# Output projection with stationary weights for 800 of its 1056 tokens

## The chip, the cores and the metric

The kernel runs on one core of a Trainium2 chip. The metric is the device time of one execution in microseconds (us); the less the better. TensorE (PE) does the matrix products, VectorE (DVE) and ScalarE (ACT) work on vectors, GpSimd (POOL) does a few element-wise operations and issues transfers, SyncE (SP) only issues transfers. PE reads a stationary operand, loaded ahead (PEld), and a moving one that streams past it, and writes to a PSUM bank of 128 partitions of 512 fp32.

## What is computed

One layer of a hybrid decoder trunk: 1024 prompt tokens and 8 x 4 = 32 sample tokens, 1056 in all, model width 1024. The end of the reference is what matters here:

```
pa = (oa * silu(ga)) @ w_proj_a      # likewise pb, pc
m = sigmoid(ma) * pa + sigmoid(mb) * pb + sigmoid(mc) * pc
hp = x + m @ w_out                   # the output projection, 1024 x 1024
y = hp * rsqrt(mean(hp * hp, axis=-1) + 1e-6) * final_norm_w
```

All is fp32. The kernel gets there with matmuls of a faster type: a matrix is split into a high part (rounded) and a low part (the rest), and a product is the sum of three: high by high, low by high, high by low.

## The kernel before

The kernel has 34 blocks of an input projection with attention and pooling beside them, then eight blocks j of 128 model columns for gates, branch products and merge, then the output projection. What runs is in the order in which it is written: each engine has its own row of instructions and follows it strictly.

In block j, gates come from `proj_chunk` (L307) in the three token pieces of `CH`, 0 to 383, 384 to 767 and 768 to 1055 (0, 384 and 768 in what follows), ACT making each a tanh (L1216, `mth`). `branch` (L1207) multiplies the branch values into a bank "s" or "t", by turns; there are two banks of each, three of "pj" and one of "o", and a bank comes free when its last reader is through. `merge_add` reads that bank on DVE (L1222), and POOL adds the outcome to the sum `m` (L1224). The last block is j = 7, its last branch br = 2: its three merges complete `m` for the eighth 128 columns.

`out_load` fetches one of the eight pieces k of the weights (`wo_raw`, 128 x 1024), `out_split` makes its high half on ACT (L1236) and its low half on DVE (L1237). Pieces 5, 6 and 7 are split after the last block. `m_split` (L1242) does the same for the tokens of `m`: copy on ACT (L1246, `mh`), difference on DVE (L1247, `ml`).

The output projection goes over nine token tiles, eight of 128 and one with the 32 sample tokens. The tokens are stationary, the weights stream by in 512 columns: 8 pieces k x 3 products x 2 halves are 48 matmuls for a tile (`out_mm`, L1342), into a bank "pj" and a bank "s". The last tile takes its columns as 512, 256 and 256, one after the other. Then DVE adds the residual (`out_part`, L1347), ACT squares with a running sum along the row (L1348), POOL makes the power of -1/2 of the mean (L1374), DVE scales by that and by the norm's weights (L1381), and SP stores.

Of the kernel before, what the change touches and what calls it, by code (L numbers as in the profile page):

```python
# [96 lines left out]
def build(tc, x_p, x_s, w_in, w_pr, w_out, nw, fnw, sink, sinkrow, w_pool, pscale, st_a, st_b1, st_b2, st_b3, st_c,  # L97
          kt_a, kt_b1, kt_b2, kt_b3, ct, c_bias, c_sb, c_pw,
          y_p, y_s, a_p, a_s, b1_p, b1_s, b2_p, b2_s, b3_p, b3_s, cp_o, cs_o):
# [1150 lines left out]
    for j in range(8):  # L1250
# [69 lines left out]
    m_split(1, range(8))  # L1320
    parts = ((mh, 0), (ml, 0), (mh, 1))
    for ti, i in enumerate(tiles):
        rows = 128 if i < 8 else NS
# [21 lines left out]
        def out_part(n, c0, cn):  # L1345
            cs = slice(c0, c0 + cn)
            dve.tensor_tensor(out=xr[:rows, cs], in0=xr[:rows, cs], in1=banks[c0][:rows, :cn], op=ALU.add)  # L1347
            act.activation(out=sq[:rows, cs], in_=xr[:rows, cs], func=AF.Square, accum_out=ss[:rows, n:n + 1])  # L1348

        dst = y_p[t0:t0 + 128, :] if i < 8 else y_s  # L1350
        if last:
            for n, (c0, cn) in enumerate(((0, 512), (512, 256), (768, 256))):
                for k in range(8):
                    for si in range(3):
                        out_mm(k, si, c0, cn)
                out_part(n, c0, cn)
                if n == 0:
                    pool.tensor_tensor(out=xr[:rows, 0:512], in0=xr[:rows, 0:512], in1=fw[:rows, 0:512], op=ALU.mult)
# [112 lines left out]
```

## Time and profile before

| | |
|---|---|
| median of 3 runs | 1087.18 us (1085.97 to 1088.93) |
| the profiled execution's own time | 1084.24 us |
| its span in the profile | 1082.5 us |
| mean granted clock of PE | 0.99 |
| busy: PE, DVE, ACT, POOL | 1045.4, 435.5, 343.9, 195.8 us |
| last gate on ACT starts | 969.37 us |
| output projection on PE | 971.98 to 1072.35 us |
| last store issued by SP | 1075.36 us |

All positions are microseconds from the start of the span. A clock of 1.00 is the upper of PE's two levels, 2.4 GHz, 0.50 the lower, 1.2 GHz. Busy shares are averages over the whole run; what a step is worth has to be read from its own stretch. On PE a matmul's own duration overlaps with that of its neighbours, so the distance from start to start is what it takes of the row.

### The profile page before, as it was taken

What the parts mean: (1) busy time and instruction counts of PE and PEld (TensorE: products, weight loads), DVE (VectorE), ACT (ScalarE), POOL (GpSimd) and SP (SyncE); (2) the same over time, 40 slices, a digit from 0 to 9 for tenths busy, and PEclk for the clock granted to TensorE, in tenths of its full rate; (3) what the DMA queues carried; (4) which work ended last, traced back from release to release, by engine and by line L of the source; (5) the groups of instructions that cost most, each with busy time, mean ns of one, the idle gap of its engine ahead of it and who ended that gap; (6) DMA issues with size and microseconds to landing.
All of it is one profiled execution on the core that took longest, in us unless ns stands there. A gap on an engine that the chain in (4) does not pass through costs nothing.

```text
span 1082.5 us, 18049 instructions
## 1 busy us (share of the span) xinstructions
PE 1045.4 (97%) x7421; PEld 994.4 (92%) x7421; DVE 435.5 (40%) x960; ACT 343.9 (32%) x888; POOL 195.8 (18%) x303
## 2 busy tenths in 40 slices
PE   7999999999999999979999899999999999999996
PEld 7998999999999999968979899999999999998884
DVE  5656654544435343474224641222122221346331
ACT  5456543544535244222211311111112121243221
POOL 5400030211303030300003460311113021111011
PEclk8999999999999999999999999999999999999998
DMA  7241133425254453527568853454143240332221
GB/s 258 79 161 59 60 126 115 149 71 184 70 176 131 124 179 113 160 80 260 194 235 208 256 167 117 164 167 136 60 135 131 83 159 33 92 116 89 100 83 58
DMA packets 54574, 144.42 MB, mean 133 GB/s; under 512 B 13030, under 2 KB 29732, under 8 KB 53156
## 3 DMA queue, kind: packets, MB, share of 16 engines
q1 hardware_dynamic: 41980, 65.28, 19.5%
q0 software_dynamic: 2816, 44.87, 12.2%
q10 hardware_dynamic: 9696, 33.12, 9.9%
q8 instruction: 58, 0.95, 0.4%
q14 instruction: 24, 0.20, 0.1%
HBM read 127.65 MB, written 60.55 MB: 174 GB/s over the span
## 4 chain that ended last, share of the span: by engine, by line
PE 83%; DMA 7%; DVE 5%; ACT 2%; POOL 1%; SPq 1%; issue 1%; POOLq 0%; ACTq 0%; DVEq 0%
PE ps_pj L307 53%; PE ps_pj L1342 5%; PE ps_s L1342 4%; PE ps_s L1207 4%; PE ps_t L1207 4%; PE ps_s L505 3%; PE ps_o L547 3%; PE ps_t L525 2%; DMA w_in<-w_scr 2%; POOL o_in L1134 1%; DMA w_raw<-in_w_in 1%; DMA w_in<-rz_scr 1%; DMA kv<-in_kt_b 1%; PE ps_o L860 1%; DMA o_in<-o_scr 1%
## 5 line engine op out<-in xcount | busy, mean ns | idle before, releaser
L307 PE MATMUL ps_pj<-xh,w_hi 128*128 128x384 f32 (+2 forms) x1408 | 461.7, 335 | 6.4 <-ACT xh L295 3.0
L307 PE MATMUL ps_pj<-xh,w_lo 128*128 128x384 f32 (+2 forms) x1408 | 443.9, 322 | 5.2 <-DVE w_lo L150 5.1
L307 PE MATMUL ps_pj<-xl,w_hi 128*128 128x384 f32 (+2 forms) x1408 | 444.4, 322 | 0.0
L307 PEld LDWEIGHTS ps_pj<-xh,w_hi 128*128 128x128 f32 x1408 | 263.2, 190 | 16.1 <-issue 6.3
L307 PEld LDWEIGHTS ps_pj<-xh,w_lo 128*128 128x128 f32 x1408 | 261.6, 188 | 6.4 <-DVE w_lo L150 6.0
L307 PEld LDWEIGHTS ps_pj<-xl,w_hi 128*128 128x128 f32 x1408 | 262.7, 189 | 0.7 <-issue 0.3
L150 DVE TENSOR_TENSOR w_lo<-w_raw,w_hi 128x1024 fp32r<-128x1024 f32 x55 | 67.3, 1224 | 204.6 <-ACT w_hi L149 197.0
L1216 ACT ACTIVATE mth<-ps_pj 128x384 f32<-128x384 f32 (+1 forms) x72 | 33.4, 464 | 257.3 <-PE ps_pj L307 250.3
L1224 POOL TENSOR_TENSOR m<-m,mth 128x384 f32<-128x384 f32 (+1 forms) x48 | 47.8, 1012 | 275.4 <-DVE mth L1222 274.9
L397 POOL TENSOR_SCALAR k<-k 64x384 fp32r<-64x384 f32 (+1 forms) x44 | 20.1, 458 | 298.4 <-ACT k L393 298.1
L512 ACT ACTIVATE e<-e,nm_b 128x256 f32<-128x256 f32 (+1 forms) x96 | 44.2, 461 | 62.9 <-DVE nm_b L509 62.6
L149 ACT ACTIVATE w_hi<-w_raw 128x1024 fp32r<-128x1024 f32 x57 | 60.1, 1054 | 1.0 <-DMA w_raw<-in_w_in 1.0
L357 DVE SCALAR_TENSOR_TENSOR q<-ps_pj,q 64x384 fp32r<-64x384 f32 (+1 forms) x60 | 30.7, 512 | 60.2 <-ACT q L356 60.1
L505 PE MATMUL ps_s<-k,q 128*128 128x256 f32 x320 | 51.6, 285 | 0.9 <-DVE nm_a L509 0.9
L505 PEld LDWEIGHTS ps_s<-k,q 128*128 128x128 f32 x320 | 45.9, 188 | 1.3 <-issue 1.2
L525 PE MATMUL ps_t<-ident,e 128*128 128x128 f32 x276 | 42.9, 273 | 1.8 <-ACT pt L530 1.1
L1134 POOL TENSOR_TENSOR o_in<-o_in,w_in 128x1024 f32<-128x1024 f32 x10 | 27.9, 2795 | 86.8 <-DMA o_in<-o_scr 62.8
L356 ACT ACTIVATE q<-ps_pj 64x384 fp32r<-64x384 f32 (+1 forms) x60 | 26.8, 447 | 50.4 <-PE ps_pj L307 29.3
L182 POOL DMA_DIRECT2D out_b_s<-in_st_b x84 | 42.2, 507 | 0.0
L512 ACT ACTIVATE e<-e,nm_a 128x256 f32<-128x256 f32 (+1 forms) x64 | 31.1, 487 | 27.9 <-DVE nm_a L509 27.9
L509 DVE CUSTOM_DVE_ANT_0 e<-ps_s,bias 128x256 f32<-128x256 f32 (+1 forms) x96 | 31.9, 371 | 14.9 <-PE ps_s L505 14.2
L525 PEld LDWEIGHTS ps_t<-ident,e 128*128 128x128 f32 x276 | 33.8, 140 | 4.3 <-ACT pt L530 1.9
(240 smaller groups left out, 1323.4 us busy)
## 6 DMA issues: line engine op xcount, KB each, us to landing
out_b_s<-in_st_b POOLq DMA_DIRECT2D x64, 511.0 KB, 6.8
w_raw<-in_w_in ACTq DMA_DIRECT2D x55, 512.0 KB
kv<-in_kt_b SPq DMA_DIRECT2D x16, 512.0 KB
kv<-in_st_b SPq DMA_DIRECT2D x16, 512.0 KB
out_b_s<-in_st_b POOLq DMA_DIRECT2D x16, 508.0 KB, 5.2
o_scr<-os SPq DMA_DIRECT2D x20, 256.0 KB
o_in<-o_scr SPq DMA_DIRECT2D x10, 512.0 KB
x_nat<-in_x_p SPq DMA_DIRECT2D x8, 512.0 KB
```

What stands on the lines that cost most here:

```text
L149: act.activation(out=hi, in_=raw, func=AF.Copy)
L150: eng.tensor_tensor(out=lo, in0=raw, in1=hi.bitcast(F32), op=ALU.subtract)
L182: pool.dma_start(out=dst, in_=src)
L307: pe.matmul(ps[:, :cn], lhsT=parts[p][0][:, k, :], rhs=parts[p][1][:, k, c0:c0 + cn], start=(step == 0), stop=(step == 23))
L505: pe.matmul(ps[:, 256 * hd:256 * hd + 256], lhsT=q, rhs=rhs, start=(i == 0), stop=(i == 1))
L512: act.activation(out=e[:, hd, :nk], in_=e[:, hd, :nk], func=AF.Exp, scale=-1.0, bias=nm, accum_out=z)
L525: pe.transpose(tp[:, o:o + 128], e[:, hd, 128 * k:128 * k + 128], ident)
L1134: pool.tensor_tensor(out=t[:, :L], in0=t[:, :L], in1=w[:, :L], op=ALU.mult)
L1207: pe.matmul(pp[:, :cn], lhsT=a[:, k, :], rhs=b[k][:, c0:c0 + cn], start=(step == 0), stop=(step == last))
L1216: act.activation(out=th[:, :cn], in_=ps[:, :cn], func=AF.Tanh, scale=0.5)
L1224: pool.tensor_tensor(out=dst, in0=dst, in1=th[:, :cn], op=ALU.add)
L1342: pe.matmul(banks[c0][:rows, :cn], lhsT=a[:, k, t0:t0 + rows], rhs=wo[k][b][:, c0:c0 + cn], start=(k == 0 and si == 0), stop=(k == 7 and s ...
```

## The change

Tokens are now in four pieces `OC`: c = 0 is tokens 768 to 1055 (288 columns, the 32 sample tokens among them), c = 1 is tokens 0 to 511, and two pieces of 128 make up the last 256.

For c = 0 and 1 the weights are stationary and the tokens stream by: for an output block o of 128 model columns, 24 matmuls (L1392) of 288 or 512 columns fill one bank. Groups of c = 0 are o = (0, 1) in the two banks "s", (2, 3, 4) in the three "pj", then 5, 6 and 7 alone in "pj"; c = 1 takes one o at a time. The result stands transposed, model columns on partitions. So the residual `x_t` comes in transposed (`x_res`), the outcome leaves as `y_t` and the host turns it back (`hand_back`). The norm is a sum over partitions: ACT squares, POOL adds the eight o up (`acc`, L1349), PE multiplies by a column of ones (L1357), DVE makes the mean, POOL the power (L1362), PE spreads it over the partitions through the identity (L1368, `spread`), ACT copies it out, DVE scales (`out_store`, L1377). The last 256 tokens go as two token tiles (L1430) like those before; the last of them, now with 128 rows and not 32, has columns 512, 256 and 256.

The low and high halves of weights 5, 6 and 7 are made earlier, in block 7, in other buffers. The last three merges go in reversed order, 768 first. The tokens' split goes by pieces of `OC`, and its first seven parts stand ahead of those merges.

```diff
+        hi = p1.tile([128, 1024], F32R, tag=t1_, name=f"wo_hi{k}", **({"bufs": 2} if p1 is wr else {}))
+        lo = p2.tile([128, 1024], F32R, tag=t2_, name=f"wo_lo{k}", **({"bufs": 2} if p2 is wr else {}))
...
+    OC = ((768, 288), (0, 512), (512, 128), (640, 128))
+
+    def m_split(c, ks):
+        s = slice(OC[c][0], OC[c][0] + OC[c][1])
         for k in ks:
             act.activation(out=mx[0][:, k, s], in_=m_t[k][:, s], func=AF.Copy)
             dve.tensor_tensor(out=mx[1][:, k, s], in0=m_t[k][:, s], in1=mx[0][:, k, s].bitcast(F32), op=ALU.subtract)
...
                 r[7] = out_load(7, wr, "whi", bufs=2)
+                out_split(5, r[5], wr, "wlo", wr, "raw")
...
+                if j == 7 and br == 2 and ci == 1:
+                    out_split(7, r[7], gh, "h3", gl, "l3")
...
                 mx[:] = [mh, ml]
+                out_split(6, r[6], wr, "wlo", wr, "whi")
+                m_split(0, range(7))
...
-            for (c0, cn), th in zip(CH, ths):
+            pieces = list(zip(CH, ths))
+            for (c0, cn), th in pieces[::-1] if j == 7 and br == 2 else pieces:
                 merge_add(j, bi, c0, cn, th, branch(n0 + 1, c0, cn, br))
-                if j == 7 and br == 2 and c0 == 0:
-                    m_split(0, range(8))
+                if j == 7 and br == 2 and c0 == 768:
+                    m_split(0, [7])
...
-    out_split(5, r[5], gc1, "c0", gc2, "d0")
-    out_split(6, r[6], gc1, "c1", gc2, "d1")
-    out_split(7, r[7], gh, "h3", gl, "l3")
...
+    fw = const.tile([128, 8], F32, name="fw")
+    sp.dma_start(out=fw, in_=fnw_t)
...
+    res, acc, rs_t = {}, {}, {}
+
+    def x_res(c, places):
+        c0, cn = OC[c]
+        o = sum(1 for k in res if k[0] == c)
+        for pl, tag, n in places:
+            t = pl.tile([128, n, cn], F32, tag=tag, name="x_res", **({"bufs": 2} if pl is wr else {}))
+            sp.dma_start(out=t, in_=x_t[o:o + n, :, 288 * c:288 * c + cn].rearrange("o p t -> p o t"))
+            for i in range(n):
+                res[c, o] = t[:, i, :], t, o - i, i == n - 1
+                o += 1
+
+    def out_add(c, o, ps):
+        c0, cn = OC[c]
+        x = res[c, o][0]
+        dve.tensor_tensor(out=x, in0=x, in1=ps[:, :cn], op=ALU.add)
+        if o == 0:
+            acc[c] = const.tile([128, 512], F32, tag="reuse", name="acc")
+            act.activation(out=acc[c][:, :cn], in_=x, func=AF.Square)
+        else:
+            q = sq2[:, o % 2, :cn]
+            act.activation(out=q, in_=x, func=AF.Square)
+            pool.tensor_tensor(out=acc[c][:, :cn], in0=acc[c][:, :cn], in1=q, op=ALU.add)
+
+    def out_norm(c):
+        c0, cn = OC[c]
+        n = -(-cn // 128)
+        ps = bank("o")
+        for i in range(n):
+            m = min(128, cn - 128 * i)
+            pe.matmul(ps[:m, i:i + 1], lhsT=acc[c][:, 128 * i:128 * i + m], rhs=ones, start=True, stop=True)
+        st = const.tile([128, 8], F32, tag="fst", name="fst", bufs=2)
+        pool.memset(st[:, 0:n], 1.0)
+        for r_, i0, i1 in ((128, 0, n),) if cn % 128 == 0 else ((128, 0, n - 1), (NS, n - 1, n)):
+            dve.tensor_scalar(out=st[:r_, i0:i1], in0=ps[:r_, i0:i1], scalar1=1.0 / D, scalar2=EPS, op0=ALU.mult, op1=ALU.add)
+        pool.tensor_tensor(out=st[:, 4:4 + n], in0=st[:, 0:n], in1=mhalf.to_broadcast([128, n]), op=ALU.pow)
+
+        def spread():
+            rp = bank("t")
+            for i in range(n):
+                m = min(128, cn - 128 * i)
+                pe.matmul(rp[:, 128 * i:128 * i + m], lhsT=st[:m, 4 + i:5 + i].to_broadcast([m, 128]), rhs=ident[:m, :m], start=True, stop=True)
+            rs_t[c] = rs2[:, c % 2, :cn]
+            act.activation(out=rs_t[c], in_=rp[:, :cn], func=AF.Copy)
+
+        return spread
...
+    def out_store(c, o):
+        c0, cn = OC[c]
+        x, t, o0, full = res[c, o]
+        dve.scalar_tensor_tensor(out=x, in0=x, scalar=fw[:, o:o + 1], in1=rs_t[c], op0=ALU.mult, op1=ALU.mult)
+        if full:
+            sp.dma_start(out=y_t[o0:o + 1, :, 288 * c:288 * c + cn].rearrange("o p t -> p o t"), in_=t)
+
+    x_res(0, [(gc1, "c0", 3), (gc1, "c1", 3), (gc2, "d0", 2)])
+    x_res(1, [(gc2, "d1", 2)])
+    spread = None
+    for c in range(2):
+        c0, cn = OC[c]
+        groups = [(0, 1), (2, 3, 4), (5,), (6,), (7,)] if c == 0 else [(o,) for o in range(8)]
+        for gi, group in enumerate(groups):
+            ps = {o: bank("s" if len(group) == 2 else "pj") for o in group}
+            for k in range(8):
+                for si, (a, b) in enumerate(parts):
+                    for o in group:
+                        pe.matmul(ps[o][:, :cn], lhsT=wo[k][b][:, 128 * o:128 * o + 128], rhs=a[:, k, c0:c0 + cn],
+                                  start=(k == 0 and si == 0), stop=(k == 7 and si == 2))
+            if c == 0 and gi < 4:
+                m_split(1, range(2 * gi, 2 * gi + 2))
+            if c == 1 and gi in (5, 6):
+                m_split(gi - 3, range(8))
+            for o in group:
+                out_add(c, o, ps[o])
+            if c == 0 and gi == 1:
+                x_res(1, [(wr, "raw", 2)])
+            if c == 1 and gi == 0:
+                spread = out_norm(0)
+                x_res(1, [(wr, "whi", 2)])
+            if c == 1 and gi == 1:
+                spread()
+            if c == 1 and 1 <= gi <= 4:
+                out_store(0, 2 * gi - 2)
+                out_store(0, 2 * gi - 1)
...
+    for i in range(2):
+        xr.append(slot_tile(i, "x_tok"))
+        sp.dma_start(out=xr[i][:, :D], in_=x_p[512 + 128 * i:640 + 128 * i, :])
+    for i in range(2):
+        t0 = 512 + 128 * i
+        last = i == 1
...
+        cols = ((0, 512), (512, 256), (768, 256)) if last else ((0, 512), (512, 512))
+        banks = [bank("pj"), bank("s"), bank("pj")][:len(cols)]
...
+        def tok_mm(n, k, si):
+            a, b = parts[si]
+            c0, cn = cols[n]
+            pe.matmul(banks[n][:, :cn], lhsT=a[:, k, t0:t0 + 128], rhs=wo[k][b][:, c0:c0 + cn],
+                      start=(k == 0 and si == 0), stop=(k == 7 and si == 2))
...
-        banks = {0: bank("pj"), 512: bank("s")}
-        if last:
-            banks[768] = bank("t")
...
-        def out_mm(k, si, c0, cn):
-            a, b = parts[si]
-            pe.matmul(banks[c0][:rows, :cn], lhsT=a[:, k, t0:t0 + rows], rhs=wo[k][b][:, c0:c0 + cn],
-                      start=(k == 0 and si == 0), stop=(k == 7 and si == 2))
...
+                    for n in range(2):
+                        tok_mm(n, k, si)
+            spread = out_norm(1)
+            for n in range(2):
+                tok_part(n)
...
+        if not last:
+            spread()
+            for o in range(8):
+                out_store(1, o)
...
+def hand_back(res):
+    y = np.asarray(res["y_t"]).reshape(D, 800).T
+    y_p = np.concatenate([y[288:], np.asarray(res["y_p"]), y[:256]]).reshape(1, L, D)
+    return (y_p, y[256:288].reshape(8, 4, D)) + tuple(res[name].reshape(full) for name, _, full in _OUTS[2:])
```

On DVE, at the end of block 7, the row of the kernel before has a merge, the splits of 128 columns, then the other two merges and a weight split:

```order
L1237 TENSOR_TENSOR wo_lo4_9297<-wo_raw_9231,wo_hi4_9296 128x1024
L1222 SCALAR_TENSOR_TENSOR mth01_6458<-mth01_6458,ps_s_9384 128x384
L1247 TENSOR_TENSOR ml_9383<-m_0_6221,mh_9382 128x128
...
L1247 TENSOR_TENSOR ml_9383<-m_7_9028,mh_9382 128x128
L1222 SCALAR_TENSOR_TENSOR mth01_6458<-mth01_6458,ps_t_9409 128x384
L1222 SCALAR_TENSOR_TENSOR mth2_6459<-mth2_6459,ps_s_9418 128x288
L1237 TENSOR_TENSOR wo_lo5_9428<-wo_raw_9259,wo_hi5_9427 128x1024
```

In the changed kernel the same place on DVE reads (`m_0` to `m_7` are the eight blocks of `m`):

```order
L1237 TENSOR_TENSOR wo_lo7_9361<-wo_raw_9302,wo_hi7_9360 128x1024
L1237 TENSOR_TENSOR wo_lo6_9393<-wo_raw_9300,wo_hi6_9392 128x1024
L1248 TENSOR_TENSOR ml_9391<-m_0_6221,mh_9390 128x288
...
L1248 TENSOR_TENSOR ml_9391<-m_6_8669,mh_9390 128x288
L1222 SCALAR_TENSOR_TENSOR mth2_6459<-mth2_6459,ps_s_9410 128x288
L1248 TENSOR_TENSOR ml_9391<-m_7_9028,mh_9390 128x288
L1222 SCALAR_TENSOR_TENSOR mth01_6458<-mth01_6458,ps_t_9421 128x384
L1222 SCALAR_TENSOR_TENSOR mth01_6458<-mth01_6458,ps_s_9430 128x384
```

The low half of weight 6 and seven splits now stand ahead of all three merges, and the merges of pieces 384 and 0 behind the eighth split.

On PE, from the last branch products into the output projection, the kernel before has:

```order
L1207 MATMUL ps_s_9418<-ghi7_5563,p_hi_9029 128x288
L1207 MATMUL ps_s_9418<-glo7_5564,p_hi_9029 128x288
L1207 MATMUL ps_s_9418<-ghi7_5563,p_lo_9030 128x288
L1342 MATMUL ps_pj_9461<-wo_hi0_9195,mh_9382 128x512
L1342 MATMUL ps_s_9462<-wo_hi0_9195,mh_9382 128x512
```

And the changed kernel, in the same place:

```order
L1207 MATMUL ps_s_9430<-ghi6_5435,p_hi_9029 128x384
L1207 MATMUL ps_s_9430<-glo6_5436,p_hi_9029 128x384
L1207 MATMUL ps_s_9430<-ghi6_5435,p_lo_9030 128x384
L1207 MATMUL ps_s_9430<-ghi7_5563,p_hi_9029 128x384
L1207 MATMUL ps_s_9430<-glo7_5564,p_hi_9029 128x384
L1207 MATMUL ps_s_9430<-ghi7_5563,p_lo_9030 128x384
L1392 MATMUL ps_s_9453<-mh_9390,wo_hi0_9195 128x288
L1392 MATMUL ps_s_9454<-mh_9390,wo_hi0_9195 128x288
```

The first matmuls of the output projection went to one bank "pj" and one "s"; they now go to the two banks "s", which hold the branch products `ps_s_9410` and `ps_s_9430` that DVE's first and last merge read.

On PE, between the last two token tiles, the changed kernel has (before, a tile's last matmul is followed by the next tile's first):

```order
L1430 MATMUL ps_s_9989<-wo_lo7_9361,mh_9390 128x512
L1357 MATMUL ps_o_10039<-ones_9441,acc_9721 128x1 x4
L1368 MATMUL ps_t_10059<-ident_71,fst_10044 128x128 x4
L1430 MATMUL ps_pj_10079<-wo_hi0_9195,mh_9390 128x512
L1430 MATMUL ps_pj_10079<-wo_hi0_9195,ml_9391 128x512
```

The sums of squares of c = 1 and the spreading of its norm came in there, four small products each.

## Rows read from the trace of the kernel before

**Rows 1.** Page, part 2: PE's busy tenths in 40 equal slices.

```profile
PE   7999999999999999979999899999999999999996
```

**Rows 2.** Stretch 1000 to 1020: us, busy (count) by engine, clock, DMA share, GB/s.

```profile
core 0: us, PE busy (x) PEld busy (x) DVE busy (x) ACT busy (x) POOL busy (x), PEclk, DMA share, GB/s
1000.00:1020.00 20.00, 20.00 (x88) 16.18 (x87) 6.20 (x18) 5.55 (x23) 1.86 (x6) 1.00 0.30 95
```

**Rows 3.** Timeline of PE: start, us, line, out<-in, count [idle before <-releaser].

```profile
965.92 0.29 PE L307 MATMUL ps_pj<-xh,w_hi 128*128 128x288 f32 x1
...
969.11 0.34 PE L1207 MATMUL ps_s<-ghi,p_hi 128*128 128x384 f32 x1
...
971.98 0.39 PE L1342 MATMUL ps_pj<-wo_hi,mh 128*128 128x512 f32 x1
...
1061.19 0.39 PE L1342 MATMUL ps_pj<-wo_hi,mh 128*32 128x512 f32 x1
...
1066.73 0.28 PE L1342 MATMUL ps_s<-wo_hi,mh 128*32 128x256 f32 x1
...
1072.23 0.28 PE L1342 MATMUL ps_t<-wo_lo,mh 128*32 128x256 f32 x1
```

**Rows 4.** Timeline of ACT from the weights' splits to the last gate.

```profile
952.03 1.05 ACT L1236 ACTIVATE wo_hi<-wo_raw 128x1024 fp32r<-128x1024 f32 x1
...
966.18 0.49 ACT L1216 ACTIVATE mth<-ps_pj 128x384 f32<-128x384 f32 x1 [3.72 <-PE ps_pj L307]
...
969.37 0.41 ACT L1216 ACTIVATE mth<-ps_pj 128x288 f32<-128x288 f32 x1 [2.70 <-PE ps_pj L307]
969.67 1.50 ACT L1246 ACTIVATE mh<-m 128x128 fp32r<-128x128 f32 x7
```

**Rows 5.** Timeline of DVE: weight split, merges, token splits, and the last scalings.

```profile
953.12 1.22 DVE L1237 TENSOR_TENSOR wo_lo<-wo_raw,wo_hi 128x1024 fp32r<-128x1024 f32 x1 [2.99 <-ACT wo_hi L1236]
...
970.43 0.56 DVE L1222 SCALAR_TENSOR_TENSOR mth<-mth,ps_s 128x384 f32<-128x384 f32 x1 [7.91 <-ACT mh L1246]
...
973.81 0.44 DVE L1222 SCALAR_TENSOR_TENSOR mth<-mth,ps_s 128x288 f32<-128x288 f32 x1
...
978.93 3.31 DVE L1247 TENSOR_TENSOR ml<-m,mh 128x128 fp32r<-128x128 f32 x16
...
1064.55 1.41 DVE L1381 SCALAR_TENSOR_TENSOR sq_o<-x_res,fss,fw 128x512 f32<-128x512 f32 x2 [2.12 <-POOL fss L1374]
```

**Rows 6.** Timeline of POOL: the first of the last merges' additions, and one power.

```profile
971.13 1.13 POOL L1224 TENSOR_TENSOR m<-m,mth 128x384 f32<-128x384 f32 x1 [10.84 <-DVE mth L1222]
...
1030.51 0.55 POOL L1374 TENSOR_TENSOR fss<-fss,mhalf 128x1 f32<-128x1 f32 x1
```

**Rows 7.** Groups by shape, POOL, 880 to 1083: count | busy us, mean ns | idle before.

```profile
L1224 POOL TENSOR_TENSOR m<-m,mth 128x288 f32<-128x288 f32 x5 | 6.0, 1200 | 0.0
```

**Rows 8.** Timeline of PE, two matmuls after an idle time of over 2 us.

```profile
611.18 0.69 PE L307 MATMUL ps_pj<-xh,w_lo 128*128 128x384 f32 x1 [2.12 <-DVE w_lo L150]
...
632.68 0.44 PE L307 MATMUL ps_pj<-xh,w_lo 128*128 128x384 f32 x1 [2.29 <-DVE w_lo L150]
```

**Rows 9.** Stretches of 1 us from 611: us, PE busy, clock, DMA share, GB/s.

```profile
611.00:612.00 1.00, 0.82 (x3) 0.59 0.82 229
...
614.00:615.00 1.00, 1.00 (x6) 0.71 0.86 147
```

**Rows 10.** Timeline of PE and its loads: small loads of transposes, a plain fp32 product.

```profile
300.74 0.53 PEld L525 LDWEIGHTS ps_t<-ident,e 128*128 128x128 f32 x4
...
484.27 0.36 PEld L943 LDWEIGHTS ps_t<-diff,wpl 128*128 128x128 f32 x2
...
484.44 0.65 PE L943 MATMUL ps_t<-diff,wpl 128*128 128x288 f32 x2
```

**Rows 11.** Stretches of 0.5 us: us, PE busy, clock, DMA share, GB/s.

```profile
965.00:965.50 0.50, 0.50 (x5) 1.00 0.41 164
...
1067.00:1067.50 0.50, 0.50 (x7) 1.00 1.01 385
...
1076.50:1077.00 0.50, 0.00 (x0) 0.50 0.67 148
```

More of the change, by code (lines that the diff above doesn't have):

```diff
@@ L1240, in build @@
     mx = []
-    def m_split(i, ks):
-        rows = 128 if i < 8 else NS
-        s = slice(128 * i, 128 * i + rows)
+    OC = ((768, 288), (0, 512), (512, 128), (640, 128))
+    def m_split(c, ks):
+        s = slice(OC[c][0], OC[c][0] + OC[c][1])
         for k in ks:
@@ new lines, in build @@
+    fw = const.tile([128, 8], F32, name="fw")
+    sp.dma_start(out=fw, in_=fnw_t)
+    ones = const.tile([128, 1], F32, name="ones")
+    pool.memset(ones, 1.0)
+    sq2 = mp.tile([128, 2, 512], F32, tag="phi", name="sq_o")
+    rs2 = mp.tile([128, 2, 512], F32, tag="plo", name="rs_o")
+    parts = ((mh, 0), (ml, 0), (mh, 1))
+    res, acc, rs_t = {}, {}, {}
[8 more added lines that the diff above has]
+                o += 1
@@ new lines, in out_store @@
+    def out_store(c, o):
[33 more added lines that the diff above has]
+                out_store(0, 2 * gi - 1)
+            if c == 1 and gi == 2:
+                x_res(1, [(gc1, "c0", 2)])
@@ new lines, in build, with tok_part @@
+    fwb = slot_tile(4, "fw_b")
+    sp.dma_start(out=fwb[:, :D], in_=bass.AP(tensor=fnw.tensor, offset=fnw.offset, ap=[[0, 128], [1, 1024]]))
+    xr = []
+    for i in range(2):
[4 more added lines that the diff above has]
+        last = i == 1
+        x = xr[i]
+        sq = slot_tile(2 + i, "sq_tok")
+        ss = const.tile([128, 6], F32, tag="fss", name="fss", bufs=2)
+        cols = ((0, 512), (512, 256), (768, 256)) if last else ((0, 512), (512, 512))
[5 more added lines that the diff above has]
+                      start=(k == 0 and si == 0), stop=(k == 7 and si == 2))
+        def tok_part(n):
+            c0, cn = cols[n]
+            cs = slice(c0, c0 + cn)
+            dve.tensor_tensor(out=x[:, cs], in0=x[:, cs], in1=banks[n][:, :cn], op=ALU.add)
+            act.activation(out=sq[:, cs], in_=x[:, cs], func=AF.Square, accum_out=ss[:, n:n + 1])
+        if last:
+            for n in range(3):
@@ L1353, in build @@
                 for k in range(8):
                     for si in range(3):
[L1355 to L1356 removed]
+                        tok_mm(n, k, si)
+                tok_part(n)
                 if n == 0:
[L1358 removed]
+                    pool.tensor_tensor(out=x[:, 0:512], in0=x[:, 0:512], in1=fwb[:, 0:512], op=ALU.mult)
                 if n == 1:
[L1360 to L1361 removed]
@@ L1362, in build @@
-            pool.tensor_scalar(out=ss[:rows, 4:5], in0=ss[:rows, 2:3], scalar1=1.0 / D, scalar2=ss[:rows, 3:4], op0=ALU.mult, op1=ALU.add)
+                    pool.tensor_tensor(out=ss[:, 3:4], in0=ss[:, 0:1], in1=ss[:, 1:2], op=ALU.add)
+                    pool.tensor_scalar(out=ss[:, 3:4], in0=ss[:, 3:4], scalar1=1.0 / D, scalar2=EPS, op0=ALU.mult, op1=ALU.add)
+            pool.tensor_scalar(out=ss[:, 4:5], in0=ss[:, 2:3], scalar1=1.0 / D, scalar2=ss[:, 3:4], op0=ALU.mult, op1=ALU.add)
         else:
@@ L1365, in build @@
                 for si in range(3):
-                    for h in range(2):
-                        out_mm(k, si, 512 * h, 512)
-            if ti + 2 < 9:
-                m_split(tiles[ti + 2], range(8))
-            for h in range(2):
-                out_part(h, 512 * h, 512)
-            pool.tensor_tensor(out=ss[:rows, 3:4], in0=ss[:rows, 0:1], in1=ss[:rows, 1:2], op=ALU.add)
-            pool.tensor_scalar(out=ss[:rows, 4:5], in0=ss[:rows, 3:4], scalar1=1.0 / D, scalar2=EPS, op0=ALU.mult, op1=ALU.add)
-        pool.tensor_tensor(out=ss[:rows, 5:6], in0=ss[:rows, 4:5], in1=mhalf[:rows], op=ALU.pow)
+                    for n in range(2):
+                        tok_mm(n, k, si)
+            spread = out_norm(1)
+            for n in range(2):
+                tok_part(n)
+            pool.tensor_tensor(out=ss[:, 3:4], in0=ss[:, 0:1], in1=ss[:, 1:2], op=ALU.add)
+            pool.tensor_scalar(out=ss[:, 4:5], in0=ss[:, 3:4], scalar1=1.0 / D, scalar2=EPS, op0=ALU.mult, op1=ALU.add)
+        pool.tensor_tensor(out=ss[:, 5:6], in0=ss[:, 4:5], in1=mhalf, op=ALU.pow)
         for h in range(2):
@@ L1469 @@
     r = _run(nc, [arrays], core_ids=[0])
-    return tuple(r.results[0][f"out_{name}"].reshape(full) for name, _, full in _OUTS)
+    return hand_back({name: r.results[0][f"out_{name}"] for name, _, _ in _OUTS})
```

48 lines of the change are left out of this document (11 added, 37 removed).

## The prediction, made before the changed kernel was run

> **What bounds the kernel now.** I read the busy slices of the page first. TensorE (PE) is at 9 in nearly every slice of the second half, so work that leaves PE shortens the run, and work put in front of PE lengthens it [rows 1]. The table of stretches says the same of the output projection: PE 20.00 of 20 us, the granted clock 1.00 (2.4 GHz), while VectorE (DVE) has 6.20, ScalarE (ACT) 5.55 and GpSimd (POOL) 1.86 [rows 2]. The other engines matter there only where PE waits for them. The timeline of PE then gives the frame: the last branch products run from 969.11, the first matmul of the output projection starts at 971.98 with no gap, and the last one at 1072.23 [rows 3]. The span ends at 1082.5, some 10 us later. The two joints, into the projection and out of it, are what the timelines of the other engines are read for.
>
> **What the change takes away.** PE's price of a matmul is the distance of starts, since neighbours overlap. Rows 3 give three: 512 columns (1061.19 - 971.98) / 384 = 0.232 us; 288 columns (969.11 - 965.92) / 24 = 0.133 us; 256 columns (1072.23 - 1066.73) / 47 = 0.117 us. The old projection lasts 1072.23 + 0.12 - 971.98 = 100.4 us. The new one has 8 x 24 matmuls of 288 columns (25.5 us), 8 x 24 of 512 (44.6), a token tile of 48 x 512 (11.1) and one of 24 x 512 and 48 x 256 (11.2): 92.4 us. So **8.0 us** less. That is the 32 sample tokens, which had a token tile of full price and now ride along as 32 of 288 columns. Each 288-column matmul loads its own weights in the old trace too, so 0.133 us already includes that.
>
> **The hand-over into the projection.** Here the change adds a wait. Both banks of the first group (the two outputs o = 0 and 1) are the two banks "s", and the last branch products sit in them: piece 768 in one, piece 0 in the other. A bank is free when the merge (L1222 on DVE) has read it. The old first tile used one "pj" bank and the "s" bank whose merge stood first in DVE's row. The new row of DVE puts in front of the merges the low half of wo 6 and seven splits of 288 columns; and the merge of piece 0 stands behind the split of k = 7, which itself waits for POOL and ACT. The second matmul of the group needs that last merge, and everything on PE is queued behind it.
>
> I walk the chain. ACT's gate of the last piece starts at 969.37 and the next ACT instruction at 969.67 [rows 4]. That next one is now the high half of wo 6, 1.05 us [rows 4]: 970.72. DVE follows 0.04 us later (953.08 to 953.12) with 1.22 us [rows 4, 5]: 971.98. Seven splits follow. One of 128 columns costs 3.31 / 16 = 0.207 us, one of 1024 about 1.2, so on a line between them 288 columns cost 0.38: 2.65 us, 974.63. The merge of 288 columns takes 0.44 [rows 5]: 975.07, and frees the first bank. POOL starts 0.14 us after a merge (970.99 to 971.13) and takes 1.13 for 384 columns [rows 5, 6]; 288 in proportion are 0.85: 976.06. ACT's copy of k = 7 and DVE's split of it, priced as 288 columns with their hand-overs, are 0.45 each: 976.96. Two merges of 384 at 0.56, less some overlap [rows 5], end at 978.0. Without the wait this second matmul would start at 972.1. PE loses **5.9 us**. The low end is 5.3, if all DVE instructions overlap as the sixteen splits did; the high end is 7.0, with POOL's addition at the 1.20 of its group's mean [rows 7] and the load of wo 5 late. That load matters because ACT now has its half of wo 5 ahead of the gates: the last bytes of the three late loads move by 965.5 [rows 11], and ACT needs 3.1 us for two halves (1.05) and two gates (0.49) before 969.37 [rows 4], so it has 0.8 us to spare.
>
> **The clock after it.** PE then sees two idle stretches of about 3 us, with one matmul between. After an idle 2.12 us at 611.18 the granted clock stood at 0.50 (1.2 GHz); after 2.29 us at 632.68 nothing of the kind is seen [rows 8]. The four slices from 611 show 0.59, 0.50, 0.50 and 0.71 (the first and the last of the four are shown) [rows 9]: the rate halved for 0.82 + 1 + 1 + 0.58 us, half of which is lost: **1.7 us**. The other end is 0. I take the loss, because the wait is longer than either of the two.
>
> **The small new work on PE.** Norms are now sums over partitions: 3 + 4 products with a column of ones, and 3 + 4 products that spread the result, all in plain fp32. The only plain fp32 product of the old trace stands twice in the row, with two weight loads, 0.36 us for the pair; four loads that run together take 0.53, so 0.13 each [rows 10]. Bounds for one product are therefore 0.26 and 0.36. I take 0.28, near the lower: PE has other work queued and the first load hides. Fourteen cost **3.9 us** (3.6 to 5.0). The Trainium skill, TensorEngine Tiling (Array Packing), Instruction Overhead, says that a matmul of one column costs as much as one of sixty. No row here shows a one-column product. As an estimate from that page, seven of them with two records each would be 0.35 us in place of 1.96, and the time 1091.0.
>
> The first set is hidden but for its own length: PE has a whole group between the sums and the spread. The second isn't: between the two token tiles PE goes from the sums to DVE to POOL's power and back with nothing in between. POOL's power took 0.55 [rows 6], the hop to it 0.14, DVE's small instruction and the drain some 0.4: **1.1 us** (0.8 to 1.6).
>
> **Two small ones.** The single group o = 5 takes a "pj" bank that the group of three has just filled, so PE waits for one DVE addition of 288 columns: **0.4 us**. The last store grows from 64 KB to 256 KB on each of two queues. Old stores of that size moved at 385 GB/s, so 512 KB take 1.4 us, where the last 128 KB took about 1 at 148 GB/s [rows 11]: **0.4 us** (0 to 1).
>
> **What is at nothing, and its cover.** The loads of the residual in columns start at 972 and are wanted from 984 on. POOL's running sums (seven per piece) have a group of PE each, 3.2 or 5.6 us. At the end DVE has eight scalings of 512 columns, 0.71 each [rows 5], in front of the last tile's additions. Counted from the end of the first token tile it is through with all but the last addition after some 13 us (6.2 for that tile's own norm, 5.7 for the scalings, 1.1 for two additions); PE's last matmul comes after 14.5 (2.2 + 1.1 + 11.2). So it just doesn't bind, and what it is late beyond 1.5 us would be paid.
>
> **Sum.** -8.0 + 5.9 + 1.7 + 3.9 + 1.1 + 0.4 + 0.4 = +5.4 us on the profiled span: 1087.9 in place of 1082.5. The profiled execution took 1084.24 us, 1.7 more than its span and 2.9 less than the median of the runs. I put the difference on the median, 1087.18: **1092.6 us**.
>
> **Rivals.** *The hand-over is covered* (not slower). If the first group got banks that nobody holds, or the merges of pieces 384 and 0 were through at 972, the two terms of 7.6 us fall away: 1085.0. For it speaks that the old kernel had no gap there; against it that the row of DVE names the merge behind eight splits. It decides from a loss of 5.5 us at the hand-over, clock included: below that the kernel isn't measurably slower. *The clock stays up*: only the wait is paid, +3.7, 1090.9. For it speaks the gap of 2.29 us without a drop; against it the length. *Dearer joints*: a second drop of the clock after the second norm (1.7), fp32 products at 0.36 (1.1), POOL at 1.20 (0.4) and a late wo 5 (0.5): +9.1, 1096.3. *The change doesn't save what it says*, were 288-column matmuls bound by their weight loads: the 24 of rows 3 run at 0.133 with one load each, so I give this nothing of its own.
>
> **How the numbers follow.** The forecast has 0.58, the clock that stays up 0.17, the covered hand-over 0.12, the dearer joints 0.13. The range 1088.5 to 1097 leaves out the covered hand-over and the far ends. A measurement of this kernel tells about 0.3%, 3.3 us, from no change. Slower than 1090.4 hold most of the forecast, two thirds of the second case and all of the fourth: 0.78. Within: 0.18. Faster than 1083.9 needs a covered hand-over and fp32 products at a fraction of my price: 0.04.
>
> **What would show it.** Right: an idle stretch of PE before the second matmul of the projection, put down to DVE's merge, near 6 us; a clock of 0.50 after it; a second gap of about 1 us before the last token tile; PE's last matmul some 5 us later than 1072.2. Wrong: the projection starting within 1 us of the last branch product; the splits of 288 columns well off 0.38 us; or the fp32 products at a tenth of a microsecond.

## The result, and the profile after

The changed kernel takes 1093.2 us (median of 7 runs, 1089.07 to 1097.38), the kernel before 1087.12 in the same runs (1084.85 to 1088.93): 1.0057 times as long, 95% interval 1.0034 to 1.008. The forecast was 1092.6, range 1088.5 to 1097.0.

The profiled span is 1090.5 us in place of 1082.5. Not all of these 8.0 us belong to the change. I count from one event that it doesn't touch, the first of the last three branch products (L1207, 969.11 before). In the changed kernel's execution it starts at 970.65, 1.54 later; an anchor as early as 917 us (a gate on ACT) shows the same shift, so it lies ahead of the changed code; in a second execution of the changed kernel (e10) the event starts at 969.12, so it differs between executions of one kernel. All stretches below are counted from this event, A in what follows. From A to PE's last matmul it was 1072.23 - 969.11 = 103.12 us [rows 3] and is 1080.10 - 970.65 = 109.45; to the span's end it was 113.4 and is 119.9.

The page of the changed kernel, parts 1 and 2 (which answers to rows 1):

```profile
PE 1045.1 (96%) x7497; PEld 1000.7 (92%) x7497; DVE 440.3 (40%) x927; ACT 340.1 (31%) x838; POOL 205.4 (19%) x301
...
PE   7999999999999999979999999999999999989995
```

PE's busy time hardly changed (1045.4 before), although 8 us of streaming left. Its row gives the loss away in one digit: the 8 near its end is the slice from 954.2 to 981.4, which holds the hand-over. The waits of PE from 960 us on, by engine and line waited for (us in total, times, longest), say where:

```profile
PE ps_s L1392 <- DVE mth L1222: 5.3, 2, 2.9
PE ps_t L1368 <- POOL fst L1362: 1.4, 1, 1.4
PE ps_pj L1392 <- DVE x_res L1342: 0.3, 1, 0.3
```

The kernel before had none of the three. The timeline of DVE at the hand-over (start, us; compare rows 5) shows the row that PE waits for:

```profile
972.30 1.22 DVE L1237 TENSOR_TENSOR wo_lo<-wo_raw,wo_hi 128x1024 fp32r<-128x1024 f32 x1 [1.88 <-ACT wo_hi L1236]
973.44 2.66 DVE L1248 TENSOR_TENSOR ml<-m,mh 128x288 fp32r<-128x288 f32 x7
976.02 0.45 DVE L1222 SCALAR_TENSOR_TENSOR mth<-mth,ps_s 128x288 f32<-128x288 f32 x1
977.91 0.46 DVE L1248 TENSOR_TENSOR ml<-m,mh 128x288 fp32r<-128x288 f32 x1 [1.44 <-ACT mh L1247]
978.29 0.55 DVE L1222 SCALAR_TENSOR_TENSOR mth<-mth,ps_t 128x384 f32<-128x384 f32 x1
978.75 0.55 DVE L1222 SCALAR_TENSOR_TENSOR mth<-mth,ps_s 128x384 f32<-128x384 f32 x1
```

And PE in the same place (compare rows 3): one matmul after the first merge, the next only after the last, then matmuls in pairs 0.48 us apart, which is 0.24 for one where 0.133 was usual.

```profile
976.61 0.37 PE L1392 MATMUL ps_s<-mh,wo_hi 128*128 128x288 f32 x1 [2.90 <-DVE mth L1222]
979.35 0.61 PE L1392 MATMUL ps_s<-mh,wo_hi 128*128 128x288 f32 x1 [2.37 <-DVE mth L1222]
979.76 0.68 PE L1392 MATMUL ps_s<-ml,wo_hi 128*128 128x288 f32 x2
980.24 0.68 PE L1392 MATMUL ps_s<-mh,wo_lo 128*128 128x288 f32 x2
```

The second joint, between the two last token tiles, on PE:

```profile
1064.02 0.95 PE L1357 MATMUL ps_o<-ones,acc 128*128 128x1 f32 x8
1066.40 1.16 PE L1368 MATMUL ps_t<-ident,fst 128*128 128x128 f32 x8 [1.43 <-POOL fst L1362]
1067.31 0.48 PE L1430 MATMUL ps_pj<-wo_hi,mh 128*128 128x512 f32 x1
```

The stretches of 0.5 us around both places (us, PE busy, clock, DMA share, GB/s) show that the granted clock fell to 0.50, the lower level, after each, for some 3.4 us:

```profile
978.50:979.00 0.50, 0.00 (x0) 0.92 1.05 371
979.00:979.50 0.50, 0.15 (x1) 0.50 1.01 389
...
982.00:982.50 0.50, 0.50 (x4) 0.67 0.28 107
982.50:983.00 0.50, 0.50 (x6) 1.00 0.09 33
1067.00:1067.50 0.50, 0.50 (x6) 1.00 0.00 0
1067.50:1068.00 0.50, 0.50 (x3) 0.66 0.00 0
...
1071.00:1071.50 0.50, 0.50 (x3) 0.92 1.03 385
```

### The profile page after: what moved, and what is told of

Its sections match the earlier page's. It is cut to its first block, busy times and chain, and to the rows that moved or that the text cites. A ratio compares the mean times of both kernels' runs of the same rounds, so it can differ in the third digit from the quotient of the medians.

```text
span 1090.5 us, 18106 instructions
## 1 busy us (share of the span) xinstructions
PE 1045.1 (96%) x7497; PEld 1000.7 (92%) x7497; DVE 440.3 (40%) x927; ACT 340.1 (31%) x838; POOL 205.4 (19%) x301
## 4 chain that ended last, share of the span: by engine, by line
PE 81%; DVE 7%; DMA 6%; ACT 3%; issue 1%; POOL 1%; SPq 1%; POOLq 0%; ACTq 0%; DVEq 0%
PE ps_pj L307 52%; PE ps_pj L1392 6%; PE ps_s L1207 4%; PE ps_t L1207 4%; PE ps_s L505 3%; PE ps_o L547 3%; PE ps_t L525 2%; PE ps_pj L1430 1%; DMA kv<-in_kt_b 1%; DMA w_raw<-in_w_in 1%; DMA w_in<-w_scr 1%; DVE w_lo L150 1%; PE ps_s L1430 1%; DMA near<-in_st_a 1%; DVE glo L1155 1%
## 5 line engine op out<-in xcount | busy, mean ns | idle before, releaser
L150 DVE TENSOR_TENSOR w_lo<-w_raw,w_hi 128x1024 fp32r<-128x1024 f32 x55 | 71.4, 1298 | 204.3 <-ACT w_hi L149 196.7
```

Source lines behind the costliest of these rows:

```text
L150: eng.tensor_tensor(out=lo, in0=raw, in1=hi.bitcast(F32), op=ALU.subtract)
```

## The experiments

Theory: the loss is made at two joints where PE stands idle (two banks held by merges that stand behind splits on DVE; a norm that goes from PE to DVE to POOL and back with nothing between) and by the clock that falls after each. Rivals: the operands come late anyway, and the clock falls for the new stream or the small products. All kernels below are the changed kernel with one edit, except where another base is named. Their medians scatter by some 0.2%, so each is read in its ratio to the kernel before and in its own trace, from A.

| kernel | ratio to before, 95% | A to 2nd matmul of the projection | A to PE's last | A to end | clock after the hand-over | after the 2nd joint |
|---|---|---|---|---|---|---|
| before | | 3.1 | 103.1 | 113.4 | 1.00 | |
| changed | 1.0057 (1.0034 to 1.008) | 8.70 | 109.45 | 119.9 | 0.50 | 0.50 |
| e10, the same again | 1.0074 (1.0046 to 1.0103) | 8.70 | 108.64 | 119.1 | 0.50 | 1.00 |
| e1 free banks | 0.9994 (0.9975 to 1.0013) | 3.0 | 101.92 | 112.3 | 1.00 | 0.50 |
| e2 merges first | 1.0014 (0.9997 to 1.0031) | 3.72 | 102.22 | 112.6 | 1.00 | 1.00 |
| e3 sums inside | 1.0057 (1.0037 to 1.0076) | 8.71 | 106.89 | 117.4 | 0.50 | no joint |
| e4 filled wait | 1.0048 (1.0031 to 1.0066) | 8.74 | 108.15 | 118.5 | 1.00 | 0.50 |
| e5 weight 6 later | one run | 6.95 | 107.41 | 117.8 | 0.50 | 1.00 |
| e6 pieces in order | one run | 6.81 | 106.19 | 116.6 | 0.50 | 1.00 |
| e7 both | 0.996 (0.994 to 0.9981) | 3.0 | 98.71 | 109.2 | 1.00 | no joint |
| e9 root of columns | 0.9955 (0.9931 to 0.9978) | 3.0 | 96.03 | 107.7 | 1.00 | no joint |
| e11 stores apart | 0.9947 (0.9923 to 0.9971) | 3.0 | 95.98 | 106.9 | 1.00 | no joint |

**Which banks (e1).**

```diff
-        groups = [(0, 1), (2, 3, 4), (5,), (6,), (7,)] if c == 0 else ...
+        groups = [(0, 1, 2), (3, 4), (5,), (6,), (7,)] if c == 0 else ...
```

> The first group of c = 0 is now o = 0, 1 and 2 in the three banks "pj" (free once ACT has read the last gates), the second o = 3 and 4 in the banks "s"; nothing else moves. Theory (held banks): PE waited because the two banks of its first group hold branch products whose merges stand behind splits on DVE. Then the projection starts within 0.5 us of the last branch product, the clock stays at 1.00, and the wait for a bank at o = 5 goes: -5.7 -1.4 -0.3 = -7.4 us against the changed kernel, about 1085.8 us, 0.999 of the kernel before. Rival (late operands): the token splits and weight 6 come too late anyway, the wait only changes its name: gain under 1.5 us, over 1091.7 us.

PE's waits are down to one row:

```profile
PE ps_t L1368 <- POOL fst L1362: 1.4, 1, 1.4
```

From A to PE's last matmul 101.92, 7.5 us less than the changed kernel, where 7.4 was expected. DVE's row is the same as in the changed kernel, and its last merge comes as late as there, 8.1 us behind A (978.75 there); nobody waits for it now. So the operands weren't late: the rival falls.

**Which order on DVE (e2).** The banks stay "s":

```diff
-                out_split(6, r[6], wr, "wlo", wr, "whi")
-                m_split(0, range(7))
...
-                if j == 7 and br == 2 and c0 == 768:
-                    m_split(0, [7])
+                if j == 7 and br == 2 and c0 == 0:
+                    m_split(0, range(8))
+                    out_split(6, r[6], wr, "wlo", wr, "whi")
```

> The first group keeps the two banks "s"; on ACT and DVE the three last merges come first, then the eight splits of 288 columns, then weight 6. Theory (held banks, and DVE's order is what holds them): the last merge ends about 0.6 us after the last branch product, PE waits about 0.9 us there and some 0.3 for the first low split, the clock stays up: -5.7 -1.4 +1.2 = -5.9 us, about 1087.3 us. Rival (the merges are late for their own sake, or weight 6 becomes the next wait at k = 6): a wait of 2 us or more at either place, and 1089 us or more.

DVE's timeline has each merge now within 0.6 us of its product:

```profile
970.44 0.45 DVE L1222 SCALAR_TENSOR_TENSOR mth<-mth,ps_s 128x288 f32<-128x288 f32 x1 [1.32 <-ACT mh L1247]
971.42 0.56 DVE L1222 SCALAR_TENSOR_TENSOR mth<-mth,ps_t 128x384 f32<-128x384 f32 x1 [0.52 <-PE ps_t L1207]
972.47 0.56 DVE L1222 SCALAR_TENSOR_TENSOR mth<-mth,ps_s 128x384 f32<-128x384 f32 x1 [0.49 <-PE ps_s L1207]
972.94 3.86 DVE L1248 TENSOR_TENSOR ml<-m,mh 128x288 fp32r<-128x288 f32 x8
```

PE waits 0.52 us, and weight 6 becomes nobody's wait. The stretch shrank by 7.2, 1.3 more than expected; 1.5 of it is the second joint's clock, which didn't fall in this execution (below). Either cure of the hand-over does; the wait needs both the held banks and the long row.

**The parts of DVE's row (e5, e6).** e5 moves the split of weight 6 behind the merges, e6 takes the reversal of the merges back:

```diff
-                out_split(6, r[6], wr, "wlo", wr, "whi")
                 m_split(0, range(7))
...
+    out_split(6, r[6], wr, "wlo", wr, "whi")
     drain()
```

> Of the changed kernel only the split of weight 6 moves, from ahead of the seven token splits to behind the merges, on ACT and DVE. From the first of the last three gates' branch products to PE's last matmul the changed kernel's trace has 109.45 us. Theory (a sum of what stands ahead on DVE): the row of DVE starts 1.9 us sooner, so does everything behind it, PE gains 1.9 us: 107.5 us, if the clock falls as before. Rival (the splits wait for ACT or the products, not for weight 6): under 0.5 us of gain.

```diff
-            for (c0, cn), th in pieces[::-1] if j == 7 and br == 2 else pieces:
+            for (c0, cn), th in pieces:
```

> Of the changed kernel only the reversed order of the last three merges is undone: 0, 384, 768. The bank of the second matmul then waits for the merge of 768, which no longer stands behind the split of k = 7. Theory: the first matmul as late as before, the second 1.75 us sooner; 107.7 us in place of 109.45, if the clock falls as before. Rival (the later split of k = 7 is the next wait): a wait of PE at k = 7, and 109 us or more.

The second matmul comes 1.75 us sooner in e5 (1.9 expected) and 1.89 sooner in e6 (1.75 expected). So of the 5.7 us some 1.8 are weight 6 and some 1.9 the merge that stands behind the split of k = 7; if the two add up, the other 2 us would be the seven splits, which no run takes out alone. The total of e5, 107.41, meets its 107.5 by chance: the clock at the hand-over stayed down longer than in the changed kernel (the stretches of 1 and 2 us below), and at the second joint it didn't fall. The total of e6, 106.19, is 1.5 us under its 107.7, for the second of these reasons.

```profile
977.00:978.00 1.00, 0.00 (x0) 0.83 1.09 391
978.00:980.00 2.00, 1.31 (x5) 0.50 0.99 362
980.00:982.00 2.00, 2.00 (x11) 0.50 0.59 129
982.00:984.00 2.00, 2.00 (x10) 0.50 0.93 348
984.00:985.00 1.00, 1.00 (x8) 0.76 0.77 295
```

**What the clock falls for (e4).** The added matmuls compute nothing that is used:

```diff
+                        if c == 0 and gi == 0 and k == 0 and si == 0:
+                            fill = bank("pj")
+                            for f in range(12 - o):
+                                pe.matmul(fill, lhsT=wo[0][0][:, 0:128], rhs=wo[1][0][:, 0:512], start=True, stop=True)
```

> Adds 12 matmuls of 512 columns before the first and 11 before the second matmul of the projection, into a bank "pj" that nobody reads: about 2.8 and 2.55 us of work where PE stood idle. Theory (the clock falls because PE was idle): the wait for DVE is as long as ever, the clock stays at 1.00 behind it, -1.4 us, about 1091.8 us. Rival (the clock falls at this place whatever PE did, for instance with the new stream of 288 columns or the transfers that begin there): 0.50 shows again and the time stays at 1093.2 us or more.

The stretches of 2 us over the filled wait and behind it:

```profile
981.00:983.00 2.00, 1.89 (x9) 1.00 1.08 383
983.00:985.00 2.00, 2.00 (x10) 1.00 1.06 383
985.00:987.00 2.00, 2.00 (x16) 1.00 1.05 405
```

The wait is as long (8.74 to the second matmul), the same 288-column stream and the same transfers (383 to 405 GB/s) follow, and the clock stays at 1.00; 1.3 us less in the trace, where 1.4 was expected. In the times that size can't be told from none. In this execution the clock stayed up where it had fallen in all five with an idle PE, so it is the idle engine, not the stream or the transfers. The kernels without the wait (e1, e7, e9, e11) have the same stream at 1.00 too.

**The second joint (e3).**

```diff
                     for n in range(2):
                         tok_mm(n, k, si)
-            spread = out_norm(1)
+                if k == 4:
+                    spread = out_norm(1)
```

> The four products that sum the squares of c = 1 (and the mean and the power behind them) are issued after k = 4 of the first token tile instead of after its end; the spreading stays between the two token tiles. Theory (the joint's cost is PE's idle time for the power and the clock that falls after it): the idle 1.43 us goes, and the clock stays at 1.00 through the last tile, 1.7 us: -3.2 us, about 1090.0 us. Rival (the clock falls because of the small fp32 products themselves): only the wait goes, -1.4 us, 1091.8 us, with 0.50 still in the rows after the spreading.

From the first token tile's start to PE's last matmul it takes 1079.35 - 1055.31 = 24.04 us, in the changed kernel 1080.10 - 1052.88 = 27.22: 3.2 less, as expected, with the small products still there and the clock at 1.00. The first set, for c = 0, stands between full groups of matmuls and left the clock at 1.00 in every kernel that has it (for e7 the stretch from 1000 to 1020 below). So small products beside other work didn't bring the clock down here; whether at the second joint the wait does it alone or together with the small products around it, no run separates. A to the last matmul gained only 2.6, since the clock behind the hand-over, down longer in this execution, cost 0.6 us more. The times show no gain (1.0057 again), where 3.2 us were expected. The next run shows that less than that was to be had on average.

**The same kernel again (e10).**

> The changed kernel once more, beside the others on one chip. Theory (the clock after PE's idle 1.43 us between the last two tiles falls in some executions and not in others): the two waits at the start of the projection again 5.3 us, the clock at 0.50 behind them, and behind the wait of 1.43 us either 0.50 or 1.00; 1.004 to 1.007 of the kernel before.

PE's waits are the same three, 5.3, 1.4 and 0.3 us. Stretches of 0.5 us behind the hand-over and behind the second joint (the last tile starts at 1066.51):

```profile
981.50:982.00 0.50, 0.50 (x4) 0.50 0.00 0
982.00:982.50 0.50, 0.50 (x4) 0.58 0.00 0
982.50:983.00 0.50, 0.50 (x6) 1.00 0.00 0
1067.00:1067.50 0.50, 0.50 (x3) 1.00 0.00 0
1067.50:1068.00 0.50, 0.50 (x4) 1.00 0.00 0
```

The clock fell again after the first, but the last tile runs at 1.00: 25.68 us from the first token tile's start, 1.54 less than the 27.22. Of the seven profiled executions with this wait of 1.43 us the clock fell in three (changed, e1, e4) and stayed in four (e2, e5, e6, e10); after the hand-over's wait of 5.3 us, or what e5 and e6 left of it, it fell in all five. The Trainium skill, TensorE: Matmul & The Clock Gate, "What's actually happening", says that where such a change of the clock falls varies from run to run of the same kernel. It speaks of a kernel's start and not of a short wait; three falls and four others in the same code fit it, no more.

**Both joints (e7).** e1 and e3 together:

> Free banks for the first group (as in e1_free_banks) and the sums of squares inside the first token tile (as in e3_sums_inside). Theory (the two joints are independent): 7.5 and 3.2 us off, 98.8 us from the last branch products to PE's last matmul in place of 109.45, no granted clock below 0.9 in that stretch, and 0.9965 of the kernel before. Rival (scatter of the runs, not the joints, made the difference between the two in their times): no faster than e1_free_banks, 0.999.

98.71 us, with 98.8 expected, PE busy in all of it, and in the times 0.996, faster than the kernel before with the interval clear of 1:

```profile
970.00:980.00 10.00, 10.00 (x73) 1.00 0.52 163
980.00:1000.00 20.00, 20.00 (x152) 1.00 0.15 57
1000.00:1020.00 20.00, 20.00 (x93) 1.00 0.00 1
1020.00:1040.00 20.00, 20.00 (x88) 1.00 0.28 88
1040.00:1060.00 20.00, 20.00 (x96) 1.00 0.24 77
1060.00:1070.00 10.00, 10.00 (x68) 1.00 0.60 224
```

The interval overlaps a little with that of e1 (0.9975 to 1.0013), so what the second joint is worth beside the first rests on the traces more than on the times.

**The small products (e8, e9, e11).** On e7's base, the sums come from two matmuls with a matrix of ones:

```diff
+        act.activation(out=hi, in_=acc[c][:, :cn], func=AF.Copy)
+        dve.tensor_tensor(out=lo, in0=acc[c][:, :cn], in1=hi.bitcast(F32), op=ALU.subtract)
...
+            pe.matmul(ps[:, :cn], lhsT=ones_r, rhs=h, start=(n == 0), stop=(n == 1))
...
+        dve.tensor_scalar(out=rs, in0=ps[:, :cn], scalar1=1.0 / D, scalar2=EPS, op0=ALU.mult, op1=ALU.add)
+        pool.tensor_tensor(out=rs, in0=rs, in1=mhalf.to_broadcast([128, cn]), op=ALU.pow)
```

> As e7_both, and the fourteen small plain fp32 products are replaced: the sums of squares are split into halves and multiplied by a 128 x 128 matrix of ones, two matmuls of 288 and two of 512 columns, which leave the sum on every partition; the power is then taken by POOL of all columns. The token splits of the last 256 tokens come earlier. Theory (the small products cost PE some 0.25 us each): 3.5 - 0.7 = 2.8 us off, 96.0 us, 0.994 of the kernel before. Rival (they are near free beside other work): no more than 0.7 us. Risk: POOL's power of 512 columns isn't in any trace so far; at over 6 us it would hold up DVE's scalings and the end.

That failed at its named risk: 1193.4 us, 1.0964 (1.0935 to 1.0992). POOL's two powers:

```profile
1015.10 46.27 POOL L1370 TENSOR_TENSOR rs_o<-rs_o,mhalf 128x288 f32<-128x288 f32 x1
1091.02 81.94 POOL L1370 TENSOR_TENSOR rs_o<-rs_o,mhalf 128x512 f32<-128x512 f32 x1 [5.37 <-DVE rs_o L1369]
```

e9 takes the root on ACT and the reciprocal on DVE instead:

```diff
-        pool.tensor_tensor(out=rs, in0=rs, in1=mhalf.to_broadcast([128, cn]), op=ALU.pow)
+        act.activation(out=rs, in_=rs, func=AF.Sqrt)
+        dve.reciprocal(out=rs, in_=rs)
```

> As e8_ones_matrix, with the power taken by a square root on ACT and a reciprocal on DVE of all columns in place of POOL. The trace of e8_ones_matrix already shows the four matmuls with the matrix of ones at 0.26 and 0.47 us for a pair. Theory (the fourteen small products cost PE 3.5 us): 2.8 us off e7_both, 96.0 us from the last branch products to PE's last matmul, 0.9935 of the kernel before. Rival (PE's gain is given back at the end, since DVE's reciprocal of 512 columns, some 3.7 us by 0.94 us for 128, stands ahead of the last tile's additions): the stretch as short, but the span's end no sooner than in e7_both.

The stretch on PE is 96.03, as the theory said (96.0), 2.7 below e7. But 1.1 of it is given back at the end, as the rival said: from PE's last matmul to the end 11.6 us in place of 10.5. In the times e9 (0.9955) can't be told from e7 (0.996). DVE's timeline shows the eight scalings and, only behind them, the last tile's first addition, and POOL's product, which waits for ACT's square of that addition, starts at 1068.17, after PE's last matmul (1067.26):

```profile
1061.36 5.38 DVE L1377 SCALAR_TENSOR_TENSOR x_res<-x_res,fw,rs_o 128x512 f32<-128x512 f32 x8
1066.66 0.67 DVE L1438 TENSOR_TENSOR x_tok<-x_tok,ps_pj 128x512 f32<-128x512 f32 x1
...
1068.17 1.27 POOL L1448 TENSOR_TENSOR x_tok<-x_tok,fw_b 128x512 f32<-128x512 f32 x1 [8.18 <-ACT sq_tok L1439]
```

e11 parts the scalings:

```diff
+                    for o in range(4, 8):
+                        out_store(1, o)
...
-                if k == 4:
+                if k == 3:
                     out_norm(1)
...
-            for o in range(8):
+            for o in range(4):
                 out_store(1, o)
```

> As e9_root_columns, with the two matmuls of the last norm one k earlier and DVE's eight scalings parted: four before and four behind the first addition of the last tile. Theory (in e9_root_columns the eight scalings, 5.38 us in a row, kept the last tile's first addition until 1066.66, and POOL's product with the norm's weights behind it set the end): the stretch on PE stays 96.0 us, from PE's last matmul to the span's end 10.4 us in place of 11.6, about 1.2 us off, 0.9945 of the kernel before. Rival (the stores' transfers, not DVE, set the end): the end stays 11.6 us behind PE.

DVE's timeline again:

```profile
1063.31 0.68 DVE L1438 TENSOR_TENSOR x_tok<-x_tok,ps_pj 128x512 f32<-128x512 f32 x1
1063.91 3.77 DVE L1377 SCALAR_TENSOR_TENSOR x_res<-x_res,fw,rs_o 128x512 f32<-128x512 f32 x4
1067.60 0.41 DVE L1438 TENSOR_TENSOR x_tok<-x_tok,ps_s 128x256 f32<-128x256 f32 x1
```

The end stands 10.9 us behind PE's last matmul; of the expected 1.2 us 0.7 came. The four later scalings took 0.94 us each on average where the eight took 0.67, and POOL's product, which now ran beside them, 1.64 in place of 1.27. They still keep the second addition until 1067.60. At 0.9947 it is the fastest kernel here; against e9 (0.9955) the gain is too small for the times to tell.

## Why the prediction was right

Its working came out term by term, with one loss that it had put into a rival:

| term | predicted | measured | from |
|---|---|---|---|
| streams | -8.0 | -7.9 | e9: 96.03 - 2.91 - 0.73 = 92.4, before 1072.23 - 971.98 = 100.25 |
| hand-over | +5.9 | +5.7 | A to 2nd matmul 8.70, e1 2.91 + 0.13 |
| clock after it | +1.7 | +1.3 to 2.6 | 2nd matmul to first sum: 32.89 here, 31.55 in e4, 33.1 to 34.1 in e3, e5, e6, e10 |
| fourteen small products | +3.9 | +3.4 | e7 less e9, 2.68, and 0.73 |
| wait for the power | +1.1 | +1.6 | last two tiles 25.68 in e10, 24.04 in e3 |
| clock after that | 0 | 0 or 1.5 | 27.22 here, 25.68 in e10 |
| wait for a bank at o = 5 | +0.4 | +0.6 | 2nd matmul to first sum 31.55 in e4; in e7 31.12 from the first, so 30.99 from the second; PE's listed wait there is 0.3 |
| last store | +0.4 | +0.1 | end behind PE's last: 10.40, before 10.27 |

With 1.3 and 1.5 for the two clocks the right column gives +6.3, and the two traces from A to the end differ by 6.5. Two traces with other clocks would give another sum: e10's gives 5.7. That the total came so close is in part luck: the terms that came out smaller than predicted make up 1.4 us, those that came out larger 2.3, and the time of one kernel scatters by 0.2%, 2 us (e10, the same kernel, stands at 1.0074).

*The hand-over.* The chain was walked rightly, link by link: seven splits 2.66 us (2.65 said), the merge 0.45 (0.44), POOL's addition 0.79 (0.85), the second matmul 8.44 us after the gate's start (8.63 said, 978.0 from 969.37). e1 and e2 show that it takes both things it rested on. The load of wo 5, the high end of that term, did hold ACT up: ACT waited for it until 964.99, and the first of the last gates came 2.5 us late against the others. But the last gate was on time, and with more slack than the 0.8 us that the prediction had counted: ACT stood idle 1.75 us just before it.

```profile
964.99 1.06 ACT L1236 ACTIVATE wo_hi<-wo_raw 128x1024 fp32r<-128x1024 f32 x1 [4.15 <-DMA wo_raw<-in_w_out]
...
970.91 0.41 ACT L1216 ACTIVATE mth<-ps_pj 128x288 f32<-128x288 f32 x1 [1.75 <-PE ps_pj L307]
```

*The clock.* I took the loss for the hand-over because the wait was longer than the two examples [rows 8], and that was right in five of five executions. The step that failed is the other joint: the sum priced its wait of 1.1 us and left the clock at its upper level, and the drop stood only in the rival of dearer joints, at 0.13. In this profile it happened, over seven profiles in three. The fall cost 1.5 us each time, so a mean of some 0.7 us belonged into the sum.

*The wait for the power.* This term was mis-sized for a plain reason: the sum took 0.55 us for POOL's power from a row of one column [rows 6], and here POOL takes it of four, 1.02 us.

```profile
1065.32 1.02 POOL L1362 TENSOR_TENSOR fst<-fst,mhalf 128x4 f32<-128x4 f32 x1 [9.35 <-DVE fst L1361]
```

*The small products.* 0.28 each was near the mark, 0.24 measured. Four sums of one column alone take 0.95 us, two records each. The rule of the Trainium skill (TensorEngine Tiling (Array Packing), Instruction Overhead), a column as dear as sixty, gave 0.35 us for seven sums as an estimate; the trace doesn't agree. The rows of the nearest plain fp32 product [rows 10] served better.

*What stood at nothing* was so: no wait of PE for the residual's loads, POOL's sums or DVE's scalings in the changed kernel. The cover of the scalings was nearly as thin as said (in e10 DVE is through with all but the last addition 12.3 us after the first tile's last matmuls, PE after 14.7); in e9, where the end of the tiles comes 2.7 us sooner and a reciprocal of 3.35 us stands ahead of them, they bind.

*The rivals.* A covered hand-over was given 1085.0; e1 has 0.9994 of the kernel before, 1086.5. The new tiling does save what it says, and was slower for what was left open at its joints: e7 mends both without touching the tiling, and turns +0.6% into -0.4%.

What stays open: why the clock falls after the same 1.43 us in some executions and not in others. No row tells the two kinds apart.

## What to carry to other kernels

Where a new stage takes over from an old one, look first at which buffers its first instructions get and what must read these before; a change that saves time within a stage can lose most of it in the row of instructions ahead of one bank. On an engine that is the bound, a step that goes out to other engines and back belongs inside other work, half a tile ahead of its use. And an idle time of that engine is to be priced twice: once as the wait, once as the slower clock that may follow.

## What the runs showed of the hardware that I had not expected

- POOL's power costs by the column: 0.55 us for one [rows 6], 1.02 for four, 46.27 for 288 and 81.94 for 512, 0.16 us a column. The kernel's way round, a few columns and small products to spread them, is cheap beside that.
- The lower clock lasted some 3.4 us in the changed kernel and some 6.8 us in e5 (977.7 to 984.5 by its stretches), with PE busy from the second matmul on in both.
- Four products of one column in plain fp32 take PE 0.95 us, more than two matmuls of 512 columns of the split type with the same sum in them (0.47 in e9).
